# Three moves in one decoder layer: when attention values are fetched back, where a third product is summed, and when the latents are squared

## The chip, the cores and the metric

The kernel runs on one core of a Trainium2 chip. The metric is the time of one execution on the device, in microseconds (us). Before the change three runs took 900.54, 901.54 and 902.39, with a median of 901.54. A core has a matrix engine (PE; PEld is its loading of weights), a vector engine (DVE), a scalar engine (ACT), a third one (POOL), and a queue engine (SP) that issues most DMA transfers. Each works through its own list of instructions in order and waits for the others by semaphores.

## What is computed

One layer on 512 tokens of width 2048, all in fp32: RMS norm, one wide input projection, eight MLA heads and eight FoX heads in parallel, each gated by SiLU, an output projection, a second RMS norm, and the residual.

```python
proj = rms_norm(x, g_pre) @ w_in
(q_lat, kv_lat, k_rope_raw, gate_mla, fq, fk, fv, f_logit, gate_fox) = split(proj)
# MLA: the latents are normalised, then expanded to heads
q  = rms_norm(q_lat, g_q) @ w_uq          # 768 -> 8 heads x 192
kv = rms_norm(kv_lat, g_kv) @ w_ukv       # 512 -> 8 heads x 256
# FoX: logits = q k / sqrt(128) + c[query] - c[key], causal softmax, times v
o = concat([mla * silu(gate_mla), fox * silu(gate_fox)]) @ w_out
return x + rms_norm(o, g_post)
```

## The kernel before

Each fp32 product is made of three matmuls. Both operands are split into a rounded part "hi" and a rest "lo", and `mm3` (L149 to L151) adds hi·hi, hi·lo and lo·hi. A weights tile (`raw`, 128 x 1024 numbers, 512 KB) is loaded by SP (`load`, L239 to L256), cast on ACT into `whi` (L276) and subtracted on DVE into `wlo` (L279). There are three buffers of each, so a cast can only start when PE, and every DMA that reads it, is done with the tile three places before. The tiles are counted through the whole program: raw62, whi62 and wlo62 belong to one tile.

Large projections are done in seven products of half size instead of eight (`p1`, `p2`, `p4`, `q6`, `g5`, `g7`, `g3`), from sums and differences of blocks. The sums of the weights are made in DRAM in the background, by copies on SP (L312) and adding copies on POOL (L309). `paced` starts one step of these every few tiles; before each copy, SP sends a *mark* (L314), a DMA of 16 words out of the current `whi` tile into the copy's target, so that the copy can't start before PE has come so far. The mark reads `whi`, and holds that buffer until it has landed.

The program is written in the order of PE's large products. Smaller work (the scores, softmax and values of the heads; the splits; the statistics of the latents) is put into a list, `todo`. A product takes one step from the list after each of its k tiles (`pump`), `wait(n)` puts n empty steps in, and `drain` does the rest of the list at the end. From that program a scheduler makes each engine's list: it may move instructions on an engine where data allow it, and it can therefore put a step somewhat ahead of or behind the place where the list has it.

The places that the change touches:

- **The FoX heads (L1254 to L1292)**, in four pairs. For each pair there is a q product (`fox_q`), a k product (`fox_k`) and then a list with the pair's scores. The scores run in the next pair's q product, and the flips (transposes, L659) and values products (L149, tile `pvf`) in the next k product. The values v were computed earlier and written to DRAM by POOL (`v_out`, L1164, tile `v_away`). `load_v` (L1135) fetches a pair's values with SP, and `split_v` splits them on ACT (tiles `fv3h`, pair 3) and DVE (`fv3l`). A fetch stands at the top of each pair's turn, ahead of its q product.
- **The scores** of a head take four blocks of queries. Each needs a bank of PSUM of the three with the tag "at", which flips also use. A bank comes free when ACT has read it into an exponential (L650, tile `pf`) or a cast (L138, `phf`).
- **The latents' products** (L1408 to L1470). Those of the latents ("l") and of the MLA gate ("m") alternate. `lat_sum` (L1378) and `lat_less` (L1382) read the banks of a product on DVE and add them into the latents (`lat`). The product `g5` sums into two banks named `gdl`; after DVE has read them, `g3` goes on summing into the same two banks, and DVE reads them again.
- **The latents' norm.** `latent` squares a latent on ACT (L1308) and sums on DVE (L1312); `latent_stats` makes a column with small matmuls (`lbk`, `lbq`, L1323), `latent_row` spreads it (`lrk`, L510 and L511), and `latent_part` scales (L1349) and splits. These run as list steps in the gate's products `q6` and `g7` (bank `gcm`, read on DVE at L1124 into `gc`).

Of the kernel before, what the change touches and what calls it, by code (L numbers as in the profile page):

```python
# [19 lines left out]
P = 128  # L20
D = 2048
S = 512
NT = S // P
# [42 lines left out]
def tile_hybrid_layer(  # L66
# [32 lines left out]
    def slot(name, dt=F32, shape=(P, 2, S)):  # L99

        return sp.tile(list(shape), dt, tag="s", name=name)

    def bank(tag, name, bufs):
        return ps.tile([P, 512], F32, tag=tag, name=name, bufs=bufs)
# [4 lines left out]
    def att_bank(name):  # L109
        return bank("at", name, 3)  # L110
# [20 lines left out]
    def in_order(*instructions):  # L131

        for i in instructions:
            tc.keep_in_program_order(i)
# [13 lines left out]
    def mm3(o, ah, al, bh, bl, first, last, **kw):  # L148
        pe.matmul(o, ah, bh, start=first, stop=False, **kw)  # L149
        pe.matmul(o, ah, bl, start=False, stop=False, **kw)  # L150
        pe.matmul(o, al, bh, start=False, stop=last, **kw)  # L151
# [137 lines left out]
    def chunk(i, ahead_load=4, ahead=2):  # L289
        upto = i + ahead_load  # L290
        if deep:
            upto = max(upto, min(i + DEEP + 2, deep[2] - 1, state["loaded"] + i % 2))
        while state["loaded"] < min(len(chunks), upto + 1):
            load(state["loaded"])
            state["loaded"] += 1
        prepare(i + ahead)
        for k in range(i + ahead + 1, min(state["loaded"], i + ahead + (3 if deep else 2))):
            join(k)
        return ready.pop(i)
# [215 lines left out]
    todo = deque()  # L515

    def pump(n=1):
        for _ in range(n):
            if todo:
                todo.popleft()()  # L520

    def wait(n):
        todo.extend([lambda: None] * n)
# [8 lines left out]
    def paced(w):  # L532

        if state["step"] <= len(bg):
            state["tiles"] += 1
            wide = 0 <= state["step"] < len(bg) and bg[state["step"]][0].shape[1] > 1024
            pace = state["pace"] * (1 + wide)
            if state["tiles"] >= pace:
                state["tiles"] -= pace
                add_step(state["step"], w[0:1, 0, 0:16].bitcast(F32))  # L540
                state["step"] += 1
# [147 lines left out]
    def enqueue_values(hs):  # L689
        steps = [(h, kb) for h in hs for kb in range(NT)]  # L690
        for i in range(len(steps) + 1):
            if i < len(steps):
                h, kb = steps[i]
                todo.append(lambda h=h, kb=kb: h.flip(kb))
            if i > 0:
                h, kb = steps[i - 1]
                todo.append(lambda h=h, kb=kb: h.values(kb))
# [97 lines left out]
    def forget_keys(both, h):  # L795

        nk, nkm = both[:, 0, :], both[:, 1, :]
        in_order(dve.tensor_scalar(out=nk, in0=nk, scalar1=-1.0, scalar2=None, op0=ALU.mult))
        for b in range(NT):
            c = slice(b * P, (b + 1) * P)  # L800
            dve.tensor_tensor(out=nkm[:, c], in0=nk[:, c], in1=mask, op=ALU.add)
        return nk, nkm, h
# [189 lines left out]
    def product(name, g, parts, o, first, last, rate=1, at=None, held=0, side=(), turned=False):  # L992


        side = deque(side)
        kk = 0

        def step(j, kk, t, hi, lo):
            if not turned:
                mm3(  # L1000
                    o[t], *parts(kk, t), hi[:, j, :], lo[:, j, :], first and kk == 0, last and kk == 7,
                    skip_group_check=True,
                )
                return
            for f in range(2):
                c = slice((2 * t + f) * P, (2 * t + f + 1) * P)
                mm3(
                    o[t][:, f * HALF : (f + 1) * HALF], hi[:, j, c], lo[:, j, c], *parts(kk),
                    first and kk == 0 and f == 0, last and kk == 7, skip_group_check=True,
                )  # L1010

        rng = list(prods[name, g])
        for i in rng[: len(rng) - held]:
            hi, lo = chunk(i)
            for j in range(2):
                if at is not None and kk == at[0]:
                    at[1]()
                for t in range(2):
                    step(j, kk, t, hi, lo)
                kk += 1  # L1020
                pump(rate)
                paced(hi)
                if side and not held and kk % 2 == 0:
                    side.popleft()()
        w = [chunk(i, ahead=0) for i in rng[len(rng) - held :]]
        if w:
            side.popleft()()
        for t in range(2):
            for m in range(2 * len(w)):
                step(m % 2, kk + m, t, *w[m // 2])  # L1030
            if w:
                finish(t, 2, o[t])
# [31 lines left out]
    def fox_k(p, wholes):  # L1064
        kb = [proj_bank(f"fk{p}{i}") for i in range(2)]
        proj_T(fox[p]["k"], [(kb[i], P, two[i]) for i in range(2)], hh, hl)
        k = []
        for i in range(2):
            t = tmp(f"fkt{p}{i}")
            dve.tensor_tensor(out=t, in0=kb[i], in1=rrow, op=ALU.mult)  # L1070
            k.append(split(t, f"fk{p}{i}"))
            whole_block(wholes, 2 + i, t)
        return k
# [55 lines left out]
        for t in range(2):  # L1129
            act.mul(to[:, t, :], o[t], col[:, t0 + t : t0 + t + 1])  # L1130

    def load_v(pair):

        both = slot(f"fv{pair}", shape=(P, NT, 256))
        nc.sync.dma_start(both, v_away[pair].rearrange("p (t c) -> p t c", t=NT))  # L1135
        return both

    def split_v(pair, both):

        tiles = v_pair(f"fv{pair}")  # L1140
        return lambda: values_into(tiles, slice(0, 256), [both[:, t, :] for t in range(NT)], True)
# [72 lines left out]
    G = two_of(att_bank, "vg")  # L1214
# [34 lines left out]
    v_room.close()  # L1249
    pp = heads_room.enter_context(tc.tile_pool(name="pp", bufs=2, reuse_waits="tile"))  # L1250
    set_pace(4.9)
    wait(4)

    heads = None  # L1254
    for p in range(4):
        vt = load_v(3 - p)
        if p:
            q, wholes = fox_q(p)
            drain()
            keys = [load_keys(2 * (3 - p) + i) for i in range(2)]  # L1260
            todo.append(split_v(3 - p, vt))
            enqueue_values(heads)
            k = fox_k(p, wholes)
            keys = [forget_keys(*a) for a in keys]
            drain()
        else:
            keys = [forget_keys(*a) for a in keys]
            later = split_v(3, vt)
        if p == 2:
            nc.sync.dma_start(gains2[0:6, :], g_q.rearrange("o (k p) -> (o k) p", p=P))  # L1270
            nc.sync.dma_start(gains2[6:10, :], g_kv.rearrange("o (k p) -> (o k) p", p=P))
            make_gcol(gains2, NK, 10)
        vs = values_of(f"fv{3 - p}")
        heads = []
        for i in range(2):
            h = 2 * (3 - p) + i
            heads.append(
                Head(
                    f"f{h}", [q[i]], [k[i]],
                    vs[i],  # L1280
                    lambda h=h: gates[h],
                    [tuple(wholes[:, 0, c * P : (c + 1) * P] for c in (i, 2 + i))], keys[i],
                )
            )
        enqueue_scores(heads, 1)
        if p == 0:
            todo.append(later)
    l4 = slot("l4b", shape=(P, NT, L4))
    nc.sync.dma_start(l4, l4_away.rearrange("p (t c) -> p t c", t=NT))
# [77 lines left out]
    def sums_wide(n):  # L1367
        return lambda kk: [oper[n, "m"][kk // 2][:, x, kk % 2, :] for x in range(2)]

    def lat_block(f, half):  # L1370
        return [raws_of[1 + 2 * f + t][:, :, half * HALF : (half + 1) * HALF] for t in range(2)]
# [4 lines left out]
    def lat_sum(to, o, add, op=ALU.add):  # L1376
        for t in range(2):
            dve.tensor_tensor(out=to[t], in0=fold(o[t]), in1=add[t], op=op)  # L1378

    def lat_less(to, o):  # L1380
        for t in range(2):
            dve.tensor_tensor(out=to[t], in0=to[t], in1=fold(o[t]), op=ALU.subtract)  # L1382
# [65 lines left out]
    product("g7", "l", sums_wide("g7"), C, False, True, side=[*f3[2:], *d3[:2]], turned=True)  # L1448
    lat_sum(lat_block(1, 1), C, pl, ALU.subtract)
    lat_less(lat_block(0, 1), C)  # L1450
    for i in range(4):
        todo.append(lambda i=i: latent(i, raw(i)))
    G = [proj_bank(f"gdl{t}") for t in range(2)]
    product("g5", "l", sums_wide("g5"), G, True, True, side=d3[2:], turned=True)
    lat_sum(lat_block(1, 1), G, lat_block(1, 1))
    product("g3", "l", sums_wide("g3"), G, False, True, turned=True)
    lat_sum(lat_block(1, 0), G, lat_block(1, 0))
    for i in range(4, 8):
        todo.append(lambda i=i: latent(i, raw(i)))
    wait(2)  # L1460
    todo.append(lambda: latent_stats(1))
    for i in range(6):
        todo.append(lambda i=i: latent_part(i))
# [240 lines left out]
    f = og_of[1, 0]  # L1704
# [29 lines left out]
    G = [att_bank(f"od{t}") for t in range(2)]  # L1734
# [48 lines left out]
```

## Time and profile before

| | |
|---|---|
| median of three runs | 901.54 us (900.54 to 902.39) |
| profiled execution, its own time | 902.61 us |
| its span, first to last instruction | 900.8 us |
| PE busy | 886.4 us, 98% |
| PEld / DVE / ACT / POOL busy | 756.8 / 677.9 / 454.3 / 65.9 us |
| mean granted clock of PE | 0.997 |
| DMA | 218.26 MB, mean 242 GB/s |

A line of the timeline gives the start, the duration, the engine, the line of the kernel, the operation, output<-inputs, the shape and the count; in brackets stands how long the engine had been idle and what ended that. A row "engine line <- releaser: total, times, longest" is from the table of waits. SPq is SP's issue of DMAs.

### The profile page before, as it was taken

What the parts mean: (1) busy time and instruction counts of PE and PEld (TensorE: products, weight loads), DVE (VectorE), ACT (ScalarE), POOL (GpSimd) and SP (SyncE); (2) the same over time, 40 slices, a digit from 0 to 9 for tenths busy, and PEclk for the clock granted to TensorE, in tenths of its full rate; (3) what the DMA queues carried; (4) which work ended last, traced back from release to release, by engine and by line L of the source; (5) the groups of instructions that cost most, each with busy time, mean ns of one, the idle gap of its engine ahead of it and who ended that gap; (6) DMA issues with size and microseconds to landing.
All of it is one profiled execution on the core that took longest, in us unless ns stands there. A gap on an engine that the chain in (4) does not pass through costs nothing.

```text
span 900.8 us, 12841 instructions
## 1 busy us (share of the span) xinstructions
PE 886.4 (98%) x4598; PEld 756.8 (84%) x4598; DVE 677.9 (75%) x1121; ACT 454.3 (50%) x837; POOL 65.9 (7%) x86
## 2 busy tenths in 40 slices
PE   9999999999989999999999999999999999999996
PEld 9988887888878888888998999788888888887885
DVE  4579995658675747667578898967978895988785
ACT  6944443334242433435455565545554676646383
POOL 1011110011211201000000000000000000000021
PEclk9999999999999999999999999999999999999998
DMA  9798799789999999896799985798762136799878
GB/s 292 226 268 256 208 325 296 241 224 307 244 285 263 256 246 246 216 246 172 258 387 396 361 276 180 150 221 196 211 148 89 62 118 212 239 325 311 271 218 247
DMA packets 125659, 218.26 MB, mean 242 GB/s; under 512 B 16378, under 2 KB 54036, under 8 KB 124572
## 3 DMA queue, kind: packets, MB, share of 16 engines
q1 hardware_dynamic: 113484, 179.47, 60.9%
q0 software_dynamic: 11376, 37.75, 21.0%
q8 instruction: 36, 0.59, 0.3%
q10 hardware_dynamic: 736, 0.22, 0.1%
q14 instruction: 27, 0.22, 0.1%
HBM read 202.72 MB, written 65.03 MB: 297 GB/s over the span
## 4 chain that ended last, share of the span: by engine, by line
PE 84%; DVE 9%; DMA 3%; ACT 2%; issue 2%; SPq 0%; ACTq 0%; DVEq 0%
PE in L585 3%; PE fk L151 3%; PE fk L149 3%; PE fk L150 3%; PE fq L149 3%; PE fq L150 3%; PE fq L151 3%; DVE wlo L279 3%; PE sm L628 2%; PE fg L149 2%; PE fg L150 2%; PE fg L151 2%; PE oa L149 2%; PE oa L151 2%; PE oa L150 2%; PE oc L149 2%
## 5 line engine op out<-in xcount | busy, mean ns | idle before, releaser
L279 DVE TENSOR_TENSOR wlo<-raw,whi 128x1024 fp32r<-128x1024 f32 (+3 forms) x217 | 256.7, 1187 | 127.5 <-ACT whi L276 119.2
L276 ACT CAST whi<-raw 128x1024 fp32r<-128x1024 f32 (+3 forms) x217 | 221.1, 1023 | 256.6 <-issue 33.5
L149 PE MATMUL fk<-h,whi 128*128 128x512 f32 x128 | 52.4, 410 | 0.0
L149 PE MATMUL fq<-h,whi 128*128 128x512 f32 x128 | 50.8, 397 | 0.0
L149 PE MATMUL fg<-h,whi 128*128 128x512 f32 x128 | 50.3, 393 | 0.0
L151 PE MATMUL fk<-h,wlo 128*128 128x512 f32 x128 | 50.2, 393 | 0.0
L150 PE MATMUL fk<-h,whi 128*128 128x512 f32 x128 | 50.1, 391 | 0.0
L151 PE MATMUL fq<-h,wlo 128*128 128x512 f32 x128 | 50.0, 390 | 0.0
L150 PE MATMUL fq<-h,whi 128*128 128x512 f32 x128 | 49.9, 390 | 0.0
L151 PE MATMUL fg<-h,wlo 128*128 128x512 f32 x128 | 49.9, 390 | 0.0
L150 PE MATMUL fg<-h,whi 128*128 128x512 f32 x128 | 49.8, 389 | 0.0
L266 DVE TENSOR_TENSOR raw<-raw,second 128x1024 f32<-128x1024 f32 x32 | 39.0, 1217 | 0.4 <-DMA second<-in_w_out_dram 0.2
L650 ACT ACTIVATE pf<-sf,stf 128x128 f32<-128x128 f32 (+3 forms) x32 | 16.7, 524 | 31.5 <-DVE stf L643 31.5
L585 PE MATMUL in<-whi,h 128*128 128x328 f32 x128 | 30.3, 324 | 0.0
L149 PE MATMUL mq<-ln,whi 128*128 128x512 f32 x72 | 28.8, 400 | 0.0
L151 PEld LDWEIGHTS fk<-h,wlo 128*128 128x128 f32 x128 | 24.0, 188 | 5.4
L151 PEld LDWEIGHTS fq<-h,wlo 128*128 128x128 f32 x128 | 24.0, 188 | 5.3
L151 PEld LDWEIGHTS fg<-h,wlo 128*128 128x128 f32 x128 | 24.0, 188 | 5.1
L150 PE MATMUL mq<-ln,whi 128*128 128x512 f32 x72 | 28.3, 393 | 0.0
L151 PE MATMUL mq<-ln,wlo 128*128 128x512 f32 x72 | 28.2, 391 | 0.0
L149 PEld LDWEIGHTS fg<-h,whi 128*128 128x128 f32 x128 | 24.0, 188 | 4.7
L150 PEld LDWEIGHTS fg<-h,whi 128*128 128x128 f32 x128 | 24.1, 188 | 4.7
(559 smaller groups left out, 2467.8 us busy)
## 6 DMA issues: line engine op xcount, KB each, us to landing
raw<-in_w_in_dram SPq DMA_DIRECT2D x96, 512.0 KB
raw<-in_w_out_dram SPq DMA_DIRECT2D x32, 512.0 KB
second<-in_w_in_dram SPq DMA_DIRECT2D x24, 512.0 KB
bmg<-awaymg SPq DMA_DIRECT2D x20, 256.0 KB
awaymg<-rmg POOLq DMA_DIRECT2D x8, 512.0 KB, 7.1
raw<-t6v SPq DMA_DIRECT2D x8, 512.0 KB
t7o<-in_w_out_dram SPq DMA_DIRECT2D x4, 1024.0 KB
t7o<-in_w_out_dram POOLq DMA_DIRECT2D x4, 1024.0 KB, 10.5
```

What stands on the lines that cost most here:

```text
L149: pe.matmul(o, ah, bh, start=first, stop=False, **kw)
L150: pe.matmul(o, ah, bl, start=False, stop=False, **kw)
L151: pe.matmul(o, al, bh, start=False, stop=last, **kw)
L266: tc.keep_in_program_order(dve.tensor_tensor(out=raw, in0=raw, in1=second, op=ALU.add))
L276: cast = act.copy(hi[:, :m], raw[:, :m])
L279: dve.tensor_tensor(out=lo[:, :m], in0=raw[:, :m], in1=hi[:, :m].bitcast(F32), op=ALU.subtract)
L585: pe.matmul(banks[t][:, :n], a[k][:, tss[t]], b[:, j, :], start=k == 0 and m == 0, stop=k == NK - 1 and m == 2,)
L628: pe.matmul(s[:, :nn], a[:, qs], c[:, :nn], start=(i == 0), stop=(i == len(pairs) - 1))
L650: act.activation(p, s[:, :n], AF.Exp, bias=st[:, 0:1], scale=unit, accum_out=st[:, 1:2])
```

## The change

It does three things.

1. **The fetch of the values.** `load_v` is divided into taking a slot of SBUF (`v_slot`) and the DMA. For the first pair the slot is taken at the same place, and the DMA becomes step 13 of the list that runs in the next q product; two of the four empty steps ahead of the scores are gone. For the other pairs slot and fetch go behind the q product and the keys' loads, and the split goes from the head of the list to behind ten steps of flips and values.
2. **Own banks for `g3` of the latents.** It sums from zero into two other banks (`gel0` with tag "at", `gel1` with tag "pv"). DVE then adds g5's banks and g3's banks into the latents separately: two additions more.
3. **Empty steps around the squares**: three ahead of the first four squares, two ahead of the next four, one instead of two ahead of the statistics.

```diff
-    def load_v(pair):
-
-        both = slot(f"fv{pair}", shape=(P, NT, 256))
+    def v_slot(pair):
+        return slot(f"fv{pair}", shape=(P, NT, 256))
+
+    def load_v(pair, both):
+
         nc.sync.dma_start(both, v_away[pair].rearrange("p (t c) -> p t c", t=NT))
         return both
...
     set_pace(4.9)
-    wait(4)
+    wait(2)
 
     heads = None
     for p in range(4):
-        vt = load_v(3 - p)
         if p:
             q, wholes = fox_q(p)
             drain()
             keys = [load_keys(2 * (3 - p) + i) for i in range(2)]
-            todo.append(split_v(3 - p, vt))
+            vt = load_v(3 - p, v_slot(3 - p))
             enqueue_values(heads)
+            todo.insert(10, split_v(3 - p, vt))
             k = fox_k(p, wholes)
...
         else:
             keys = [forget_keys(*a) for a in keys]
+            vt = v_slot(3)
             later = split_v(3, vt)
...
         enqueue_scores(heads, 1)
         if p == 0:
+            todo.insert(12, lambda vt=vt: load_v(3, vt))
             todo.append(later)
...
     lat_less(lat_block(0, 1), C)
+    wait(3)
     for i in range(4):
         todo.append(lambda i=i: latent(i, raw(i)))
     G = [proj_bank(f"gdl{t}") for t in range(2)]
     product("g5", "l", sums_wide("g5"), G, True, True, side=d3[2:], turned=True)
     lat_sum(lat_block(1, 1), G, lat_block(1, 1))
-    product("g3", "l", sums_wide("g3"), G, False, True, turned=True)
+    G3 = [att_bank("gel0"), bank("pv", "gel1", 1)]
+    product("g3", "l", sums_wide("g3"), G3, True, True, turned=True)
     lat_sum(lat_block(1, 0), G, lat_block(1, 0))
+    lat_sum(lat_block(1, 0), G3, lat_block(1, 0))
+    wait(2)
     for i in range(4, 8):
         todo.append(lambda i=i: latent(i, raw(i)))
-    wait(2)
+    wait(1)
     todo.append(lambda: latent_stats(1))
```

What SP issues at the first pair's turn, before the change (fv3 and fv2 are the values of pairs 3 and 2, whi59 to whi61 and raw62 to raw64 weights tiles, t7l, t6l and t7m targets of background copies; a row "t7l3<-whi59" is a mark):

```order
L256 DMA raw62_2258<-in_w_in_dram 128x4x256
L1135 DMA fv3_2205<-v_away3_228 128x1024
L1135 DMA fv2_2224<-v_away2_227 128x1024
L256 DMA raw63_2312<-in_w_in_dram 128x4x256
L314 DMA t7l3_124<-whi59_2230 1x16
L314 DMA t6l3_128<-whi60_2260 1x16
L314 DMA t7m0_137<-whi61_2314 1x16
L312 DMA t7l3_124<-in_w_in_dram 128x2x512
L256 DMA raw64_2369<-in_w_in_dram 128x4x256
```

And the same place after it:

```order
L256 DMA raw62_2264<-in_w_in_dram 128x4x256
L314 DMA t7l3_124<-whi59_2227 1x16
L1137 DMA fv3_2215<-v_away3_228 128x1024
L256 DMA raw63_2321<-in_w_in_dram 128x4x256
L312 DMA t7l3_124<-in_w_in_dram 128x2x512
L314 DMA t6l3_128<-whi60_2266 1x16
L314 DMA t7m0_137<-whi61_2323 1x16
L312 DMA t6l3_128<-in_w_in_dram 128x2x512
L256 DMA raw64_2375<-in_w_in_dram 128x4x256
```

The fetch of pair 3 has moved behind one mark only; that of pair 2 is gone from here (it follows two loads of keys further on), and the other two marks still come behind the fetch and raw63. On ACT the cast into whi62 moves behind two more exponentials.

The second place is DVE between the gate's products q6 and g7 (wlo133 and wlo134 are the first two weights tiles of g7, `gc12<-gcm0` and `gcm1` the reads of q6's banks, lrkl, lrkdl and `ls<-lrk` the latents' row). Before:

```order
L1336 TENSOR_TENSOR latk_y_5418<-latk_y_5418,rcol_210 128x4
L279 TENSOR_TENSOR wlo134_5479<-raw134_5270,whi134_5478 128x1024
L139 TENSOR_TENSOR lrkl_5430<-latk_y_5418,lrkh_5429 128x4
L1124 SCALAR_TENSOR_TENSOR gc12_5518<-gcm0_5362,hcol_222,gpa_4245 128x512
L502 TENSOR_SCALAR lrkdl_5434<-ident_92,lrkl_5430 128x128 x4
L1124 SCALAR_TENSOR_TENSOR gc12_5518<-gcm1_5363,hcol_222,gpa_4245 128x512
L512 COPY ls_3918<-lrk_5491 128x512
```

After:

```order
L1340 TENSOR_TENSOR latk_y_5422<-latk_y_5422,rcol_210 128x4
L139 TENSOR_TENSOR lrkl_5434<-latk_y_5422,lrkh_5433 128x4
L502 TENSOR_SCALAR lrkdl_5438<-ident_92,lrkl_5434 128x128 x4
L1124 SCALAR_TENSOR_TENSOR gc12_5522<-gcm0_5366,hcol_222,gpa_4245 128x512
L1124 SCALAR_TENSOR_TENSOR gc12_5522<-gcm1_5367,hcol_222,gpa_4245 128x512
L279 TENSOR_TENSOR wlo133_5450<-raw133_5242,whi133_5449 128x1024
L279 TENSOR_TENSOR wlo134_5480<-raw134_5272,whi134_5479 128x1024
L512 COPY ls_3918<-lrk_5501 128x512
```

Both divisions (wlo133 stood further ahead, between the latents' parts) now come behind the two reads. On ACT the casts whi133 and whi134 go behind lrkdh in the same way, and the cast whi136 goes ahead of the last latent's cast. PE's own list is the same set of matmuls, with the scores up to two k tiles earlier.

## The prediction

> **What bounds the kernel now.** I read the page's busy table first, then what PE waited for, then the busy time by stretches, and last the timelines of the engines around each wait of PE. The page says that PE is busy nearly all the time, at full clock.
>
> ```profile
> span 900.8 us, 12841 instructions
> PE 886.4 (98%) x4598; PEld 756.8 (84%) x4598; DVE 677.9 (75%) x1121; ACT 454.3 (50%) x837; POOL 65.9 (7%) x86
> ```
>
> So only PE's own waits and the kernel's two ends can be won. In the table of waits (us in total, times, longest), PE's list is short:
>
> ```profile
> PE sf L628 <- ACT pf L650: 1.2, 1, 1.2
> PE gdl L149 <- DVE lat L1378: 1.1, 1, 1.1
> PE ptf L659 <- ACT pf L650: 1.1, 1, 1.1
> ```
>
> These three lie where the change works. Behind the first two PE has no gap for a long time, as a stretch of the windows shows (length, then PE's busy time):
>
> ```profile
> 270.00:414.00 144.00, 144.00 (x693) 119.83 (x692) 91.42 (x202) 52.79 (x115) 16.92 (x19) 1.00 0.95 244
> ```
>
> A microsecond won at 256 us is therefore passed on to the end, unless something that feeds PE becomes late.
>
> I size the waits from start to start, since a matmul's busy time overlaps the next one's.
>
> ```profile
> 242.99 0.69 PE L628 MATMUL sf<-fk,fq 128*128 128x384 f32 x3
> 243.51 0.40 PE L149 MATMUL fq<-h,whi 128*128 128x512 f32 x1
> ...
> 254.18 0.39 PE L151 MATMUL fq<-h,wlo 128*128 128x512 f32 x1
> 254.51 0.80 PE L628 MATMUL sf<-fk,fq 128*128 128x384 f32 x3
> 256.56 0.95 PE L628 MATMUL sf<-fk,fq 128*128 128x512 f32 x3 [1.25 <-ACT pf L650]
> 257.34 0.39 PE L149 MATMUL fk<-h,whi 128*128 128x512 f32 x1
> 257.57 0.39 PE L150 MATMUL fk<-h,whi 128*128 128x512 f32 x1
> ...
> 261.67 0.40 PE L151 MATMUL fk<-h,wlo 128*128 128x512 f32 x1
> 263.18 0.55 PE L659 MATMUL ptf<-ident,pf 128*128 128x128 f32 x3 [1.12 <-ACT pf L650]
> ...
> 538.72 0.28 PE L150 MATMUL gdl<-bmg,whi 128*128 128x256 f32 x1
> 538.84 0.28 PE L151 MATMUL gdl<-bmg,wlo 128*128 128x256 f32 x1
> 540.26 0.35 PE L149 MATMUL gdl<-bmg,whi 128*128 128x256 f32 x1 [1.14 <-DVE lat L1378]
> ```
>
> Three scores matmuls of 384 columns take 0.52 us unhindered (242.99 to 243.51) and took 2.05 at 254.51: 1.53 lost. A 512-column matmul takes 0.23 (257.34 to 257.57) and the gap at 261.67 is 1.51: 1.28 lost. A 256-column one takes 0.12 (538.72 to 538.84) and the gap at 538.84 is 1.42: 1.30 lost.
>
> **The first two waits: the values' fetch.** The scores wait for ACT's exponentials (pf), and ACT was held up:
>
> ```profile
> 252.73 1.05 ACT L276 CAST whi<-raw 128x1024 fp32r<-128x1024 f32 x1 [6.19 <-DMA t7l<-whi]
> ...
> 262.46 0.58 ACT L650 ACTIVATE pf<-sf,stf 128x384 f32<-128x384 f32 x1 [1.17 <-DVE stf L643]
> ```
>
> ACT stood 6.19 us at the cast into whi62, until the DMA "t7l<-whi" had landed. That is the pacing mark (L314), which reads 16 words of whi59, the buffer that whi62 overwrites. Why it was late is seen in the view of the fetch's own line (its waits in ns, shortest, median, longest) and in SP's timeline:
>
> ```profile
> L1135 SPq EVENT_SEMAPHORE  x4: 17/642/9302, 234.1 to 243.9; - x4
> ```
>
> ```profile
> 233.68 0.39 SPq L256 DMA_DIRECT2D raw<-in_w_in_dram  x1
> 243.52 2.04 SPq L1135 DMA_DIRECT2D fv<-v_away  x2
> 245.60 0.68 SPq L256 DMA_DIRECT2D raw<-in_w_in_dram  x1
> 246.33 0.81 SPq L314 DMA_DIRECT2D t7l<-whi  x1
> ```
>
> SP reached the first values' fetch at 234.1, stood 9.3 us for the values' write to DRAM, and the mark behind it left at 246.33. In the changed order the mark stands ahead of the fetch, right behind raw62: it can leave at 234.1 and, at the 6.40 us it took from issue to the cast (246.33 to 252.73), is done by 240.5. The cast into whi62 then waits only for the two exponentials that now go ahead of it. The input of the larger one stands ready at 248.9 today already:
>
> ```profile
> 248.21 0.69 DVE L643 TENSOR_REDUCE stf<-sf 128x1 f32<-128x512 f32 x1
> ```
>
> With about 0.7 and 0.4 for the two the cast comes at 250, and nothing on ACT stands for SP. The fetch itself is not twelve tiles later on SP: it still stands there at 234 and still waits until 243.5, with raw63 behind it, which today leaves at 245.60 and then at 244.1. So the gain comes from the one mark that gets ahead, and from the second fetch that is gone from this place.
>
> The first wait (1.53) should go wholly: the bank that PE waits for comes free with the second of these exponentials, at 250 instead of behind a cast that began at 252.73. For the second (1.28) I follow DVE from the end of the q product to the exponential whose bank the flip takes. Today:
>
> ```profile
> 257.60 0.68 DVE L1059 SCALAR_TENSOR_TENSOR fqt<-fq,rrow 128x512 f32<-128x512 f32 x1
> ...
> 261.30 0.61 DVE L639 SCALAR_TENSOR_TENSOR sf<-sf,ccol,nk 128x128 f32<-128x128 f32 x2
> 261.82 1.14 DVE L643 TENSOR_REDUCE stf<-sf 128x1 f32<-128x384 f32 x2
> ```
>
> From fqt to the exponential at 262.46 it takes 4.86 us. After, q ends at 254.6 as today (254.18 + 0.39) and fqt can start at 254.7, 2.9 us earlier; the exponential ends 262.46 + 0.58 - 2.9 = 260.1 if that chain keeps its length, and about 258.8 if it shortens, since in the new order the last score's steps (half of the two x2 rows, 0.3 and 0.6, and a first step of some 0.5) come behind it. PE wants that bank 12 fk matmuls of 0.23 and one flip of some 0.4 after fk's start at 255.8 (257.34 less 1.53), at 259.0. So 0 to 1.2 us of waiting stays. Behind it the split of the values, which stood last on ACT, holds the first values matmul perhaps 0.5 (0 to 0.6). I take 0.6 of both, as the order shows the shorter chain. Gain 2.81 - 0.6 = **2.2 us** (1.0 to 2.8).
>
> [...]
>
> The fetches for pairs 2, 1 and 0 move behind the keys' loads at the end of q, with ten more steps before their split. Each is one issue, half of the 2.04 us that the two took, and delays the weights load behind it by that; I cost it at nothing, since such a load goes out long ahead of its cast (raw62 at 233.68 for 252.73), and at 1.0 us each if that cover were gone. The split (three casts and a copy on ACT, three subtractions on DVE per pair) only changes place behind the k product's matmuls, which have no gap there.
>
> **The third wait: own banks.** g3 goes to gel0 and gel1, so PE need not wait until DVE has read g5 out of gdl; 1.30 goes. What is next late there is the second half of a weights tile (wlo); it was ready at 539.44, when DVE went over to lat. PE wants it a weights tile of 24 matmuls later, at 538.96 + 24 x 0.12 = 541.8, so nothing new waits: **1.3 us** (0.7 to 1.3). That the squares come three tiles later costs PE nothing: only the statistics read them, more than a product later, and casts of weights get ahead of them on ACT. The two more additions (lat<-gdl) cost DVE 2 x 0.64 from the first row, hidden in an idle time like that of the second, of which there are two more; if it weren't there, the squares would come 1.3 later.
>
> ```profile
> 539.44 1.28 DVE L1378 TENSOR_TENSOR lat<-gdl,lat 128x512 f32<-128x512 f32 x2
> ...
> 547.24 1.23 DVE L279 TENSOR_TENSOR wlo<-raw,whi 128x1024 fp32r<-128x1024 f32 x1 [1.61 <-ACT whi L276]
> ```
>
> **The latents' tail (q6 to g7 of the gate).** Here the new order costs and gains.
>
> ```profile
> 563.53 0.74 DVE L1124 SCALAR_TENSOR_TENSOR gc<-gcm,hcol,gpa 128x512 f32<-128x512 f32 x1
> 564.19 0.86 DVE L502 TENSOR_SCALAR lrkdl<-ident,lrkl 128x128 fp32r<-128x128 f32 x4
> ```
>
> ```profile
> 563.74 0.49 PE L510 MATMUL lrk<-lrkdh,ones 128*128 128x512 f32 x1
> 564.33 0.50 PE L149 MATMUL gcm<-whi,bmg 128*128 128x512 f32 x1
> ...
> 573.98 0.39 PE L151 MATMUL gcm<-whi,bmg 128*128 128x512 f32 x1
> 574.82 0.74 PE L149 MATMUL gcm<-whi,bmg 128*128 128x512 f32 x2 [0.45 <-ACT whi L276]
> 575.77 0.74 PE L149 MATMUL gdm<-whi,bmg 128*128 128x512 f32 x2 [0.21 <-ACT whi L276]
> 576.34 0.40 PE L150 MATMUL gcm<-wlo,bmg 128*128 128x512 f32 x1
> ```
>
> DVE today divides the first two tiles of g7 (wlo133, wlo134) before it reads q6's banks; after, it does so behind both reads. In today's clock the two reads start at 563.53 and 564.19, the division at 564.85, and it ends at 566.08 (1.23, as at 547.24). By then PE has issued nine instructions today (the lrk at 563.74, and eight from 564.33 on, 0.23 to 0.33 apart) and after only four (two lrk, and two matmuls that need no wlo): five times 0.23, **1.1 us lost**, and by the same shift some 0.4 at the third tile, an estimate. Against that, the fourth tile's cast (whi136) now stands ahead of the last latent's cast, so the gaps at 574.82, 575.77 and 576.34 (0.84 - 0.23, 0.95 - 0.46, 0.57 - 0.23: together 1.44) and 0.3 of the wait ahead of 564.33 go. Net 1.74 - 1.5 = **0.2 us** gained (1.2 lost to 1.4 gained).
>
> **Sum.** 2.2 + 1.3 + 0.2 = 3.7 us. The profiled execution took 902.61, of which 1.8 lie outside its span; it would take 898.9. The median of the three runs is 901.54, 1.1 below, and the same 3.7 gives 897.8. Ends: 2.8 + 1.3 + 1.4 = 5.5 and 1.0 + 0.7 - 1.2 = 0.5.
>
> **Rivals.** *The next mark takes the place.* The cast into whi63 needs whi60's mark, which stands behind the fetch, raw63 and a t7l load. At 9.2 us from 243.5 it lands at 252.7; PE lets whi60 go at 254.6, a margin of 1.9 us. If it lands later than that, ACT stands again with the last two exponentials behind the cast, and the second wait comes back whole with 1 us more at the values: gain 1.5 + 1.3 + 0.2 - 1.0 = 2.0, that is 899.5, and less with each microsecond that the mark is later. For: the fetch still stands there. Against: the margin, and one of the two fetches is gone.
>
> *The tail of the latents loses.* If the gaps at 574.82 and after stay and the losses come, the third term is -1.5: with 2.2 + 1.3 that is a gain of 2.0, and with a second wait of 1.2 left, of 1.4: 899.5 to 900.1.
>
> *Slower: the old wait three times over.* The fetches of pairs 2, 1 and 0 now stand at the end of q with a weights load right behind each. If each stands there for its slot as the first did for its write (9.3 us), it costs what the first cost, 2.8 us each: 8.4 - 3.7 = 4.7 slower, 906.2. It decides once a fetch stands over some 6 us. For: a fetch ahead of a weights load on SP is just what hurt. Against: the key loads stand at the same place today and appear in no row of SP's waits, and the slots that they take were read by scores that are over.
>
> **Chances.** Forecast 0.70, the next mark 0.14, the latents' tail 0.10, slower 0.06. A measurement can tell about 0.2%, 1.8 us: below 899.7 is faster. The forecast's own spread leaves 0.05 within it, and the two middle rivals lie at the edge, a third of them faster: faster 0.72, same 0.21, slower 0.07. Range 896.0 (the upper end of the gains) to 901.0 (the lower end, which takes in both middle rivals).
>
> **What would show it.** Right: SP's mark t7l at 234 to 235, ahead of the fetch; ACT without a wait for t7l or t6l; PE at 257 without a gap, and at most 1.2 us at the flip; gel starting 0.12 after gdl; a new gap of about 1 us after q6 with gc or wlo named, and none at 574. Wrong: a wait of ACT for t6l<-whi, a row of SP's waits for L1137 with three long ones, a gap of 2 us or more at g7, or a time above 901.

## The result, and the profile after

Twelve executions of the changed kernel have a median of 899.33 us (897.76 to 901.19), twelve of the kernel before, beside them, 902.46. The ratio is 0.9965, with a 95% interval of 0.9955 to 0.9976: 3.2 us faster (2.2 to 4.1). The changed kernel, timed a second time, gave 0.9953 (0.9936 to 0.9969). The profiled execution took 897.76 us, the shortest of the twelve. One execution of a kernel below (own banks alone) took 1258.44 us where its ten others took 899.7 to 902.0; its ratio is without it.

The page of the changed kernel, its span and busy table:

```profile
span 896.0 us, 12851 instructions
PE 883.9 (99%) x4598; PEld 755.2 (84%) x4598; DVE 678.7 (76%) x1123; ACT 453.8 (51%) x837; POOL 65.7 (7%) x86
```

In its table of waits the three rows of PE that the prediction began with (sf, gdl and ptf) are gone, and at the places of the change one row is new:

```profile
PE gcm L150 <- DVE wlo L279: 0.6, 1, 0.6
```

SP's timeline after, at the first values' fetch: the mark leaves at 234.25, ahead of the fetch, which still stands until 243.41.

```profile
234.25 0.48 SPq L314 DMA_DIRECT2D t7l<-whi  x1
243.41 0.32 SPq L1137 DMA_DIRECT2D fv<-v_away  x1
243.78 0.43 SPq L256 DMA_DIRECT2D raw<-in_w_in_dram  x1
...
245.68 0.48 SPq L314 DMA_DIRECT2D t6l<-whi  x1
...
252.20 0.56 SPq L312 DMA_DIRECT2D t6l<-in_w_in_dram  x1
```

The last row is a copy that waits for the second mark, so that mark had landed by 252.2. ACT's casts into whi62 and whi63 in the same timeline wait for no DMA: the first stands behind an exponential, the second 0.15 us for PE.

```profile
249.55 1.04 ACT L276 CAST whi<-raw 128x1024 fp32r<-128x1024 f32 x1
...
253.78 1.05 ACT L276 CAST whi<-raw 128x1024 fp32r<-128x1024 f32 x1 [0.15 <-PE fq L150]
```

And PE goes through both places without a gap: six scores matmuls in 1.22 us, and the flip 0.26 behind the last fk matmul.

```profile
253.80 1.38 PE L628 MATMUL sf<-fk,fq 128*128 128x384 f32 x6
255.02 0.40 PE L149 MATMUL fk<-h,whi 128*128 128x512 f32 x1
...
258.00 0.40 PE L151 MATMUL fk<-h,wlo 128*128 128x512 f32 x1
258.26 0.55 PE L659 MATMUL ptf<-ident,pf 128*128 128x128 f32 x3
```

The four fetches, by their own line (shortest, median and longest, in ns): one waits, 8.55 us for the write of the values. The three that moved behind the keys' loads wait 17 to 28 ns at their semaphores; the issue of the last of them takes 1.43 us, and SP's table of waits puts 1.4 of that down to PE's flips.

```profile
L1137 SPq EVENT_SEMAPHORE  x6: 17/17/8546, 234.8 to 364.6; - x6
```

At the latents, g3 begins 0.12 us after g5's last matmul:

```profile
535.44 0.28 PE L151 MATMUL gdl<-bmg,wlo 128*128 128x256 f32 x1
535.56 0.28 PE L149 MATMUL gel<-bmg,whi 128*128 128x256 f32 x1
```

From q6 to g7, PE's timeline and then DVE's. The two divisions (a double row of 2.35 us) stand behind the two reads (1.44), and PE waits for the first of them:

```profile
559.41 1.03 PE L149 MATMUL gcm<-whi,bmg 128*128 128x512 f32 x2
561.08 0.50 PE L150 MATMUL gcm<-wlo,bmg 128*128 128x512 f32 x1 [0.64 <-DVE wlo L279]
...
567.60 0.38 PE L1396 MATMUL gmt<-ident,gc 128*128 128x128 f32 x2
568.13 0.50 PE L150 MATMUL gcm<-wlo,bmg 128*128 128x512 f32 x1
```

```profile
558.46 1.44 DVE L1124 SCALAR_TENSOR_TENSOR gc<-gcm,hcol,gpa 128x512 f32<-128x512 f32 x2 [0.97 <-PE gcm L151]
559.81 2.35 DVE L279 TENSOR_TENSOR wlo<-raw,whi 128x1024 fp32r<-128x1024 f32 x2
```

From 559.41 to 561.08 two matmuls of 0.23 took 1.67: 1.21 lost, where 1.1 was forecast. At 567.60 two small flips took 0.53; the first two took 0.31 in the profile before (571.50 to 571.81, below), 0.22 less. The gaps of before at 574 to 576 have no counterpart.

```profile
571.50 0.38 PE L1392 MATMUL gmt<-ident,gc 128*128 128x128 f32 x2
571.81 0.50 PE L150 MATMUL gcm<-wlo,bmg 128*128 128x512 f32 x1
```

**Where the time came from.** PE issues the same matmuls in both kernels, so the trace can be cut at three pairs of PE's rows: the first stretch holds the scores and the flip, the second g5 and g3 of the latents, the third the gate's q6 and g7. Before, the first stretch runs from 130.41 to 286.54; after:

```profile
129.76 0.39 PE L149 MATMUL vg<-whi,smg 128*128 128x512 f32 x1
...
283.00 0.47 PE L149 MATMUL fq<-h,whi 128*128 128x512 f32 x1
```

| stretch (us) | before | after | gained |
|---|---|---|---|
| first vg to the third pair's first fq | 156.13 | 153.24 | 2.89 |
| first gdl to first gcm | 24.40 | 23.04 | 1.36 |
| first gcm to first mq | 38.88 | 38.76 | 0.12 |

Together that is 4.4 of the 4.8 us between the two spans; 0.65 more lies ahead of the first vg (130.41 against 129.76), where no edit reaches, and some 0.4 was lost behind these stretches. The 4.4 is also more than the 3.2 that the twelve executions show. The experiments had to settle which is right, and why.

### The profile page after: what moved, and what is told of

Same layout as the page of the kernel before. It is cut to its first block, busy times and chain, and to the rows that moved or that the text cites. A ratio compares the mean times of both kernels' runs of the same rounds, so it can differ in the third digit from the quotient of the medians.

```text
span 896.0 us, 12851 instructions
## 1 busy us (share of the span) xinstructions
PE 883.9 (99%) x4598; PEld 755.2 (84%) x4598; DVE 678.7 (76%) x1123; ACT 453.8 (51%) x837; POOL 65.7 (7%) x86
## 4 chain that ended last, share of the span: by engine, by line
PE 85%; DVE 8%; DMA 3%; ACT 2%; issue 1%; SPq 0%; DVEq 0%; ACTq 0%
PE fk L149 3%; PE fk L151 3%; PE fq L149 3%; PE fk L150 3%; PE fq L151 3%; PE fq L150 3%; PE in L585 3%; PE sm L628 2%; DVE wlo L279 2%; PE fg L149 2%; PE fg L150 2%; PE fg L151 2%; PE oa L149 2%; PE oa L151 2%; PE oa L150 2%; PE mq L149 2%
## 6 DMA issues: line engine op xcount, KB each, us to landing
t7o<-in_w_out_dram POOLq DMA_DIRECT2D x4, 1024.0 KB, 10.2
```

## The experiments

**The three edits, each alone.** First the fetch:

```diff
-    wait(4)
+    wait(2)
...
+            todo.insert(12, lambda vt=vt: load_v(3, vt))
```

with the rest of the first edit as in the change.

> The kernel before with only the first edit (the values' fetches moved, two empty steps fewer ahead of the scores). Theory: the marks and exponentials alone remove both waits of PE at 254.5 and 261.7 us (1.53 + 1.28 = 2.81 lost before), and nothing else changes: PE still loses 1.3 at g3 of the latents and about 2.2 from q6 to g7. Time 2.2 to 2.8 us under before, ratio 0.9970 to 0.9975. Rival: part of what the whole change showed comes from the start of the kernel, which no edit touches (0.6 us less in its profile), and the gain is 2 us or under.

Measured: 0.9983 (0.9974 to 0.9991), that is 1.5 us (0.8 to 2.3), so under the 2.2 to 2.8 that theory gave. Yet in its trace the first stretch lasts 153.24, as in the changed kernel: nothing of the wait is left. So either the kernel before doesn't lose 2.8 on most executions, or the edit costs something elsewhere; the looks at the kernel before further down decide. The start of the kernel can't be the whole answer either: it gave 0.65 in one pair of profiles and scattered from 129.57 to 131.04 over all kernels here.

```diff
-    product("g3", "l", sums_wide("g3"), G, False, True, turned=True)
+    G3 = [att_bank("gel0"), bank("pv", "gel1", 1)]
+    product("g3", "l", sums_wide("g3"), G3, True, True, turned=True)
     lat_sum(lat_block(1, 0), G, lat_block(1, 0))
+    lat_sum(lat_block(1, 0), G3, lat_block(1, 0))
```

> The kernel before with only g3 of the latents summed into its own two banks. Theory: the gap of 1.30 us at the first matmul of g3 goes, nothing takes its place, and the gaps from q6 to g7 stay as before (about 2.2 in all), since DVE's and ACT's orders there are those of before. Ratio about 0.9986. Rival: the two more additions on DVE make a weights tile late within g3 and give some 0.6 of it back, ratio 0.9992.

Measured: 0.9982 (0.9973 to 0.9991), 1.6 us. The second stretch is 23.04 instead of 24.40, the third 38.89 as before: the theory, and no sign of the rival.

```diff
+    wait(3)
     for i in range(4):
         todo.append(lambda i=i: latent(i, raw(i)))
...
+    wait(2)
     for i in range(4, 8):
         todo.append(lambda i=i: latent(i, raw(i)))
-    wait(2)
+    wait(1)
```

> The kernel before with only the empty steps around the squares. Theory: these steps alone, not the banks, put the two divisions behind the reads of q6's banks: a gap of 1.1 to 1.3 us at g7's second weights part appears, and the gaps at 574 to 576 (0.61, 0.49, 0.34) go; g3's 1.30 and the fetch's 2.81 stay. Time within 0.3 us of before. Rival: the reads stand in another place for the banks' sake, and this kernel keeps the gaps of before.

Measured: 1.0005 (0.9992 to 1.0019), no difference that can be told. The steps alone put the divisions behind the reads, and the third stretch is the changed kernel's (38.75). Its table of waits has the same new row, and a longer wait ahead of g3, which shares its banks with g5 here:

```profile
PE gdl L149 <- DVE lat L1378: 1.6, 1, 1.6
...
PE gcm L150 <- DVE wlo L279: 0.6, 1, 0.6
```

The 1.6 was 1.1 before: the squares' sums stand elsewhere on DVE, and the read of g5's banks comes half a microsecond later. With own banks nobody waits for it.

**One more empty step.** With two in place of one ahead of the statistics, DVE has g7's first two divisions ahead of both reads of q6's banks (in its trace they start at 554.69 and 557.92, the reads at 559.06 and 559.80).

```diff
-    wait(1)
+    wait(2)
     todo.append(lambda: latent_stats(1))
```

> The changed kernel with two empty steps instead of one ahead of the statistics of the latents. DVE then divides g7's first two weights tiles ahead of and between the reads of q6's banks and the latents' row comes six weights parts later. Theory: the gap of 1.2 us at g7 goes (0.3 left, for the first read) and the gaps at 574 to 576 do not come back: 1.0 to 1.4 us under the changed kernel, ratio to before about 0.9952. Rival: what was gained is lost where the latents are next needed, since their row and their casts are later: a wait of PE on ln or on wlo at the end of g7 or in the first query product, 0.5 us or more, and no gain over the changed kernel.

Measured: 0.9965 (0.9951 to 0.9979), no gain over the change, and the third stretch is 39.97, 1.2 longer. PE's timeline shows the rival: the wait for a division has moved to the end of g7, where DVE now has the latents' parts and a read of g7's banks ahead of it.

```profile
573.89 0.73 PE L149 MATMUL gdm<-whi,bmg 128*128 128x512 f32 x2
575.37 0.50 PE L150 MATMUL gdm<-wlo,bmg 128*128 128x512 f32 x1 [0.74 <-DVE wlo L279]
```

**What of the fetch's edit does it.** Each of the next four kernels was profiled once (times of 900.09, 902.06, 899.40 and 899.15, beside 902.44 of before), so the first stretch of each is compared. In the first of them the first fetch stays at the top and the four empty steps stay; only the fetches of pairs 2, 1 and 0, and their splits, move:

```diff
-        vt = load_v(3 - p)
         if p:
...
+            vt = load_v(3 - p, v_slot(3 - p))
...
         else:
             keys = [forget_keys(*a) for a in keys]
+            vt = load_v(3, v_slot(3))
```

> The kernel before with only the fetches of pairs 2, 1 and 0 moved behind q: the first fetch stays at the top, ahead of raw63 and of the mark, and the four empty steps stay. ACT's order is that of before (cast whi62 ahead of two exponentials). If the mark lands behind what goes ahead of it at 3.07 us per 512 KB from 243.5 (theory: the transfers count), then with two transfers instead of three it lands at 249.6, ACT casts whi62 some 3 us earlier than before, the gap of 1.53 goes and of 1.28 at most 0.5 stays. If it takes 6.40 us from its own issue (rival), it lands at 251 and PE keeps 0 to 0.3 of the first gap and 0.5 or more of the second. If only the mark's place ahead of the fetch helps (the forecast's wording), most of the 2.81 stays.

Measured: the first stretch lasts 153.08, with nothing lost at either place, although the mark leaves behind the fetch and behind raw63. SP's timeline, and then ACT's:

```profile
243.31 0.32 SPq L1137 DMA_DIRECT2D fv<-v_away  x1
243.73 0.38 SPq L256 DMA_DIRECT2D raw<-in_w_in_dram  x1
244.15 0.36 SPq L314 DMA_DIRECT2D t7l<-whi  x1
...
248.18 0.56 SPq L312 DMA_DIRECT2D t7l<-in_w_in_dram  x1
```

```profile
248.26 1.05 ACT L276 CAST whi<-raw 128x1024 fp32r<-128x1024 f32 x1 [2.25 <-PE fq L151]
```

The copy of 248.18 waits for the mark, which so landed 4.87 us after the fetch had left, with two transfers of 512 KB ahead of it; before it was 9.21 with three. Theory gave 249.6 (its 3.07 us per 512 KB is a third of the 9.21), its rival 251: it was earlier than both, and ACT waited for PE only. So in this execution taking the second fetch away was enough; that the mark gets ahead of the first one was not needed. Mark and PE were ready within 0.1 us of each other. The cast led the 256-column scores (252.43) by 4.17 us; by the line found below, a lead under some 2.8 would begin to cost, so the margin was 1.4 us, an estimate that goes beyond the leads measured there.

```diff
-    wait(4)
+    wait(2)
```

> The kernel before with two empty steps instead of four ahead of the first scores, and the fetches where they were. SP's order is that of before, so the mark lands at about 252.7 and ACT stands for it again, but two exponentials now go ahead of that cast. Theory A (what hurts PE is the exponentials behind the cast): the gap of 1.53 goes without any move of the fetch, and of the 1.28 some 0 to 1 stays, since the casts of the q product and the next exponential still follow a late cast. Theory B (the mark is what counts): ACT's order doesn't help, and 2 us or more of the 2.81 stay.

Measured: the gap at the scores is gone, but the first stretch lasts 155.27. ACT casts whi62 at 251.06, again behind the mark. What is late next are the values: on ACT their split stands behind the last score's exponential, which waited 2.49 us for DVE, itself behind since that cast. PE waits 1.65 us.

```profile
251.06 1.05 ACT L276 CAST whi<-raw 128x1024 fp32r<-128x1024 f32 x1 [2.67 <-DMA t7l<-whi]
...
262.13 0.69 ACT L650 ACTIVATE pf<-sf,stf 128x512 f32<-128x512 f32 x1 [2.49 <-DVE stf L643]
```

```profile
263.25 0.50 PE L149 MATMUL pvf<-phf,fv3h 128*128 128x512 f32 x1 [1.65 <-ACT fv3h L138]
```

Theory A was right about the scores, which the exponentials ahead of the cast save. By the sum theory B was right: 2.0 us are lost (155.27 less 153.24), no less than the 1.8 that the other kernels with the fetch of before lose on the mean (below), and the delay only comes out a few microseconds further on. The mark is what counts.

The change's fetch with `wait(4)` kept:

> The first edit with the four empty steps kept: SP's order is that of the changed kernel (mark ahead of the first fetch, second fetch gone), ACT's cast whi62 stands ahead of two exponentials as before. Theory: the mark is done by 241, ACT has no wait for it, and both gaps (1.53 and 1.28) go. Rival: with the exponential of the last score now behind the casts of the q product on ACT, PE waits 0.3 to 1 us at a score or a flip.

Measured: 153.06 for the first stretch, no wait of PE at scores, flips or values. The rival didn't show. With the two runs before it this says that the two empty steps earn nothing once the mark is early.

```diff
-            todo.insert(12, lambda vt=vt: load_v(3, vt))
+            todo.insert(16, lambda vt=vt: load_v(3, vt))
```

> The first edit with the first fetch four steps further on in the list, which puts it behind raw63, raw64, raw65 and all three marks on SP. SP then doesn't stand at 234 for the values' write, raw63 leaves at 234 and not at 244. Theory: PE's two gaps go as in the changed kernel and nothing more is gained, since nothing on ACT stood for SP there; the values come later but are split only at 261. Rival: the fetch comes too late for the split, and PE waits 0.5 us or more at the first values product.

Measured: 153.17, as theory had it. The fetch leaves SP at 256.00 and its values are there when ACT comes to split them at 260.82. On SP the theory was too hopeful: raw63 left at 238.94, not at 234.

**The kernel before, looked at twice more.** This was the question that the first two runs left: they had the fetch of before, and lost less there.

> The kernel before, unchanged, looked at again. Theory: what PE loses at the two waits behind the values' fetch is set by when the mark lands against PE's place, and that differs from execution to execution: loss = 2.8 us + (start of the cast whi62 - start of the last head's 256-column scores), so that it is 2.8 only where the cast starts with those scores, and 1.2 to 1.7 where it starts 1.2 to 1.6 ahead of them, as in the two runs that had the fetch of before. Rival: this kernel loses 2.81 each time, and the smaller losses came from the edits of those two runs.

> The kernel before, unchanged, a third time. Theory: as for the second look, the loss behind the values' fetch lies between 1 and 2.9 us and follows the cast's start one for one, within 0.2. Rival: 2.81 again.

Measured: the theory. The second look, ACT and then PE, whose scores now run in one piece while the flip still waits:

```profile
251.10 1.05 ACT L276 CAST whi<-raw 128x1024 fp32r<-128x1024 f32 x1 [4.96 <-DMA t7l<-whi]
```

```profile
252.56 0.52 PE L628 MATMUL sf<-fk,fq 128*128 128x256 f32 x3
254.30 1.59 PE L628 MATMUL sf<-fk,fq 128*128 128x384 f32 x6
...
261.55 0.55 PE L659 MATMUL ptf<-ident,pf 128*128 128x128 f32 x3 [1.09 <-ACT pf L650]
```

The cast leads those scores by 1.46 us, where it started 0.07 behind them in the profile that the prediction read. Over the five executions with the fetch of before and the four empty steps (the loss is the first stretch less 153.24):

| execution | cast less scores | first stretch | lost |
|---|---|---|---|
| before, first profile | +0.07 | 156.13 | 2.89 |
| before, third look | -1.15 | 154.92 | 1.68 |
| own banks alone | -1.18 | 154.85 | 1.61 |
| before, second look | -1.46 | 154.62 | 1.38 |
| empty steps alone | -1.58 | 154.50 | 1.26 |

A cast that is 1.65 us earlier loses 1.63 less: one for one. What changes is the wait at the scores: 1.25 in the profile that was read, 0.24 and 0.22 in the third look and with own banks, no wait of its own in the other two. The wait at the flip is there each time, 1.07 to 1.12. Yet both hang on the cast, for in all five the flip starts 10.44 or 10.45 us after it. The mean loss of the five is 1.8, and the profile that was read is the highest of them. Two things differ in it: the fetch left 9.14 us ahead of those scores instead of 9.9 to 10.2, since the write that it waits for landed later, and the mark took 9.21 us from there to the cast instead of 8.5 to 8.8. Why the DMA was slower that time isn't settled. The five don't all come from one chip; but on one chip the fetch left 112.03 us after the first vg in the kernel with the fetch alone (at 241.60) and 113.34 in that with one more empty step (at 243.04), so the write's landing scatters without a change of chip.

**The moves that seemed to do the work, without the others**: the late fetch, own banks, no empty steps at the squares.

> The kernel before with the first fetch truly late (behind raw65), the other three behind q, and g3's own banks, but none of the empty steps around the squares: what the experiments point to as the same gain by fewer moves. Theory: no loss behind the fetch, none at g3, and from q6 to g7 the 2.2 us of before: within 0.5 us of the changed kernel (which loses 2.4 there), ratio to before about 0.9963. Rival: the empty steps earn something that no gap of the single executions shows, and this is 1 us or more slower than the changed kernel.

Measured: 0.9970 (0.9959 to 0.9980). The theory missed. Its trace loses 1.6 us where the same fetch lost nothing in the run above: the values left SP at 256.49 and came 1.16 us too late for ACT.

```profile
262.91 1.02 ACT L138 CAST fv3h<-fv 128x256 fp32r<-128x256 f32 x3 [1.16 <-DMA fv<-v_away]
```

```profile
PE pvf L149 <- ACT fv3h L138: 1.4, 1, 1.4
```

So a fetch that late has no sure cover, and the change's place for it, one mark later and no more, is the safer one. The third stretch is 38.90 against the changed kernel's 38.76, so the empty steps are not what is missed here.

> The changed kernel again, for a second interval and a second look on the same chip as the combination. Theory: ratio 0.996 to 0.9975; no gap at the scores and under 0.5 at the flip, 1.1 to 1.3 us at g7. Rival: the 4.8 us of the first pair of profiles is what it is worth, ratio 0.995 or lower.

Measured: 0.9953 (0.9936 to 0.9969), with stretches of 153.26, 23.04 and 38.69, and no wait at scores or flip. That is 4.2 us (2.8 to 5.8) under before, between the theory's ratios and the rival's 0.995; the interval holds both, so it decides nothing between them. The median is 2.2 us under that of the combination, timed beside it (897.71 to 899.93): the size of the combination's rival, though the two intervals overlap and 1.6 of it is seen at the values.

## Why the prediction was right, and where it was not

- **The sum and its sign.** 3.7 us were forecast. From 902.46, which is the median of before over twelve executions, that makes 898.8, and 899.33 was measured; 897.8 rested on a median of three, which lay 0.9 lower.
- **First term, forecast 2.2, the one that was mis-sized.** Its mechanism held in each step: the mark ahead of the fetch, the cast with no DMA to wait for, the scores without a gap. The second wait went wholly, where 0.6 was left standing for flip and split together (in the run with one more step 0.4 stayed). The exponential that the flip needs ended at 258.1 (257.52 + 0.59), which is 258.8 on the clock of the profile before (0.65 later), as the forecast's shorter chain had it; the half microsecond that was put down for the split of the values didn't come. But the 2.81 that it was taken from was one execution's, the worst of five, and what was untypical in it is the 1.53 at the scores; the 1.28 at the flip is there each time. Against their mean of 155.00 the four traces with the change's fetch (153.24, 153.26, 153.24 and 153.75) gain 1.6. That agrees with the 1.5 timed for this edit alone.
- **A reason that fell.** The prediction said that the gain comes from the one mark that gets ahead of the fetch, and from the second fetch that is gone. The second alone did it in the one run that has it alone.
- **Second term, 1.3.** The stretch gained 1.36, and the edit alone 1.6 (0.8 to 2.4). The two more additions cost PE nothing.
- **Third term, 0.2.** 0.12, as the balance of two effects that were each seen: 1.21 lost at the divisions (1.1 forecast), 0.22 at the third tile (0.4 forecast), against the gaps at 574 to 576. The run with the steps alone shows that they, not the banks, do both.
- **With these sizes** 1.6, 1.36 and 0.12 make 3.1, and 3.2 was measured. That 3.7 came so near is in part luck: the loss was read too large by 1.0 and what would be left of it by 0.5. The second timing's 4.2 is 1.1 more than the three sizes hold; its interval reaches down to 2.8, so that anything is missing isn't shown, nor excluded. The 4.8 between the two profiles needs no other cause than a bad execution of before and 0.65 us of the start.
- **PE's list of waits** was not only the three rows that the prediction shows. The longest row, 2.2 us for ACT ahead of the products named mix, lies at the end of the kernel and is 2.2 after the change too.
- **The next mark** held nobody in any trace of the change's fetch: it landed by 252.2, and PE let its buffer go at 253.7, 1.5 us later (1.9 forecast). The 9.2 us that the forecast counted with are the time from the first fetch to the cast in the profile that it read (243.52 to 252.73). **The latents' tail** neither lost nor gained. **The slower rival** is out: of the three fetches that moved one took 1.43 us, the others under 0.4, where the rival needed over 6 us.
- **What a mark waits behind.** It took 8.5 to 9.2 us from the first fetch to the cast with three transfers of 512 KB ahead of the mark (six executions), and 4.87 to the copy with two (one execution). Two thirds of 9.21, 6.1, would be the estimate for the two, and is more than the 4.87 measured. What holds the mark behind them, no run here shows.

## What to carry to other kernels

A wait on a DMA in one profile is one draw: before pricing its removal, look at the kernel before two or three times (2.89, 1.38 and 1.68 us lost here), and size the wait by where the landing falls against the engine that waits. A small transfer that holds a buffer should not queue behind large ones (here a mark of 16 words behind three of 512 KB kept ACT waiting 4.84 to 6.19 us in the five executions of the table), and to take one large transfer away can be enough (no wait for the mark with two). Where a list of small steps only changes which of two late things is late, expect the sum to stay (38.75 us with the empty steps alone, 38.88 before).

## What was not expected of the hardware

Executions of one program differ by over a microsecond in two places at least (1.5 us at the values' fetch, 1.04 at the MLA heads), and in both ACT stands at the cast of a weights tile. The two stretches in which no wait for a DMA is on PE's path repeated to 0.05 us: the second was 24.40, 24.41 and 24.40 in three looks at the kernel before, the third 38.88, 38.91 and 38.87. The stretch with the values' fetch scattered by 1.5. A wait of PE for the exponentials of the MLA heads scattered too, here in the second look at the changed kernel, against 0.4 in the first:

```profile
PE sm L628 <- ACT pm L650: 1.4, 1, 1.4
```

It follows a cast as well. In four traces the time from one head's 512-column scores to the next head's 256-column ones grows one for one with the start of ACT's cast of a weights tile: the cast comes 0.02 us after the former and the step takes 3.98 in the kernel before, 0.28 and 4.23 in the changed one, 0.49 and 4.44 in the second look at the kernel before, 1.32 and 5.27 in the second look at the changed one. Here is the cast in the kernel before and in that second look:

```profile
622.59 1.05 ACT L276 CAST whi<-raw 128x1024 fp32r<-128x1024 f32 x1 [1.10 <-DMA raw<-in_w_ukv_dram]
```

```profile
619.57 1.05 ACT L276 CAST whi<-raw 128x1024 fp32r<-128x1024 f32 x1 [2.41 <-PE sm L628]
```

In the first and second look at the kernel before, the row names the load of that weights tile (idle 1.10 and 1.57 us); in both looks at the changed kernel (1.36 and 2.41) and with the fetch alone (2.50) it names PE's scores, so what held the cast there isn't settled. With the fetch moved and the steps kept, and in the combination, PE has no wait there and the step is 3.58. This one wait, 1.0 us apart between two looks at one kernel, is a third of what the change is worth.
